# A new order for the opening's steps, a third pair run ahead, and the sums of the right factors on other ground

## The chip, the cores and the metric

One NeuronCore of a Trainium2 chip runs the whole program. The metric is the device time of one execution in microseconds (us); lower is better. The kernel before took 1624.2 us, the median of three runs from 1623.47 to 1624.24.

## The reference, cut to what matters

The program is one inference step of a one-layer streaming encoder on 1024 prompt rows and 8 x 16 sample rows, 1152 rows of 1024 channels in all. What the change touches is its first part, the norm and the input projection:

```python
def rmsnorm(x, g):
    xf = x.astype(jnp.float32)
    y = xf * lax.rsqrt(jnp.mean(xf * xf, axis=-1, keepdims=True) + EPS)
    return (y * g.astype(jnp.float32)).astype(x.dtype)

h = rmsnorm(x, g_pre_mix)
p = h @ w_in          # 1024 x 4352: queries, keys and values of two attentions, and two gates
```

Behind it come two attentions with position biases (two small tables are spread out in memory for them at the start), their projections, the gates, and a gated MLP. Those parts are the same in both kernels.

## The kernel before, in words

**Numbers in two parts.** Each fp32 operand of a matrix product is split into a high and a low part of a reduced format, so a product is three: high x high, high x low, low x high. ACT makes the high part (a copy), DVE the low part (a subtraction).

**The input projection** works on pairs of output tiles (`pairs`, twelve of them) with a scheme of Strassen's kind: seven products of half size stand in for eight, on sums of the halves of the weights (left factors, `left_factors`, L127 to L133) and of the input (right factors, `right_factors`, L429 on). The normed input, transposed, has channels on partitions; its halves by channels and by rows are b11, b12, b21 and b22, and t1, t2, t3 and t4 are the sums. A half has 576 rows, worked on as two chunks of 256 and 320 columns. One product of one left factor with one right factor and one chunk is twelve matmuls (`chunk_product`, L143).

**The opening** (L262 to L404). SP loads the nine blocks of 128 input rows (L279), with the left halves of the weights of the first two tiles among them (L285, behind blocks 1 and 3); seven buffers hold the nine blocks, so blocks 7 and 8 wait for the norms of blocks 0 and 1. For each block: `square` (ACT squares and sums, L296; DVE and GpSimd make the factor, L96 and L97), `norm` (DVE, L303 or L306), `transposed` (eight transposes on PE, L314, into two PSUM banks), `high` (ACT, L330) and, for rows of the first half, `low` (DVE, L335). Blocks 0 and 1 fill the first chunk of b11 and b21, blocks 2, 3 and half of 4 the second; the rest goes to b12 and b22 as plain fp32. The gains are spread over the partitions by PE, and `gp` is their copy by ACT (L350).

**The far products.** For the first tile of each of the first seven pairs, the two products with b11 and b21 are done ahead by the class `Away`: it splits the two left factors (L176, L177), `run(i, c)` is one product (i = 0 with b11, then i = 1 added onto it, chunk c), `copy(i, c)` copies the sum so far to `ia0h` or `ia1h` (L251), which are stored (L255, L195). `run(1, c)` waits for `copy(0, c)`. Tiles 0 and 1 are done within the opening, tile 2 (`Away(2)`) right behind it, tiles 3 to 6 after the pools of the opening are closed.

**What sets the order.** Within the opening the order on ACT, DVE and PE is written out by hand (`manual_schedule`). SP and GpSimd, and everything else in the program, are put in order by the framework's planner, which goes by dependencies and by its own estimates of times; each engine's and each queue's order is then fixed. Memory is a stack of pools: what is allocated after a pool is closed lies on the same addresses, and each tile waits for the last use of what lay beneath it (`reuse_waits="tile"`).

**The right factors.** After the opening, with its pools closed (input rows `xt` lowest, then `xn`, then small tables: `gp`, `eb`, `oh`, and `ea` last), the pools t3, t2, t1 and t4 are laid down in this order (L427). `sums` (plain fp32 for t3, t2 and t1) has the place that t4 takes later. `right_factors` is a generator of six steps: the sum for t3 with its parts; the sums for t1 and t2 (L438) with t2's parts (L211, L212); t1's parts; b22's parts; t4's sums (L438, L461) and parts; b12's parts. The first step is issued ahead of tiles 3 to 6, the others one by one in the first `tail`.

**The tail of a pair** (`tail`, L486): the product z with t3, x with t2, x with t1, x with b22, z with t4, each with the next left factor, which DVE sums in place in the raw weights `iw` (L127 to L133; loaded at L217) and ACT and DVE split (L176, L177, written `s_i`, `a_i`); in between DVE adds and copies out (`iu`, `iv`, `iw`, L191).

**After it** comes attention. Its first allocations on the same side are two buffers of raw rows (`karaw`, `q0raw`, ... loaded at L583), then four of bias tables, then the split rows of q and k. PE has dense gate tiles (`d`, L117 to L119) to fill in between the scores (`s`, L697).

Of the kernel before, what the change touches and what calls it, by code (L numbers as in the profile page):

```python
# [11 lines left out]
F32 = mybir.dt.float32  # L12
F32R = mybir.dt.float32r
# [5 lines left out]
P = 128  # L19
# [33 lines left out]
def encoder_step(ctx, tc, x, w_in, w_o, w_out, w_upg, w_down, kc, vc, state_conv, conv_w, conv_b,  # L53
# [104 lines left out]
    def chunk(c):  # L158
        return slice(c * widths[0], widths[0] + c * widths[1])
# [3 lines left out]
    with ExitStack() as ph:  # L163
# [7 lines left out]

        b12, b22 = [rq.tile([P, 4, 2 * CW], F32, name=n) for n in ("b12", "b22")]

        def split_left(src, name):
            sp = wop.tile([P, 2, 4, P], F32R, name=name, tag="wop")
            nc.scalar.activation(sp[:, 0], src, AF.Copy)  # L176
            nc.vector.tensor_tensor(sp[:, 1], src, fr(sp[:, 0]), op=ALU.subtract)  # L177
            return sp

        def two_chunks(name):  # L180
            return pa.tile([P, 2 * CW], F32, name=name, tag="a")

        def copy_out(ps, t):
            for c in range(2):
# [49 lines left out]
        class Away:  # L234


            def __init__(self, f, pool, early=False):
                self.f, self.pool, self.early = f, pool, early
                raw = away_weights(f)
                self.left = [split_left(raw[:, 4 * i:4 * i + 4], f"ih1{i}_{f}") for i in range(2)]  # L240
                self.out = [two_chunks(f"ia{i}h{f}") for i in range(2)]
                self.ps = [None, None]

            def run(self, i, c):
# [19 lines left out]
        with ExitStack() as pre:  # L264
# [73 lines left out]
            b = []  # L338

            def enter():  # L340
                b.append(Block(len(b)))
                b[-1].square()

            with tc.manual_schedule(engines={mybir.EngineType.Activation, mybir.EngineType.DVE, mybir.EngineType.PE}):
                enter()
                b[0].norm()
                enter()
                b[0].transposed()
                for i in range(2):
                    nc.scalar.activation(gp[:, i * 512:(i + 1) * 512], gps[i][:], AF.Copy)  # L350
                b[1].norm()
                b[0].high()
                b[0].low()
                w0 = Away(0, psx, True)
                b[1].transposed()
                b[1].high()
                b[1].low()
                enter()
                w0.run(0, 0)
                b[2].norm()  # L360
                w0.copy(0, 0)
                w1 = Away(1, psx, True)
                enter()
                b[2].transposed()
                b[2].high()
                w0.run(1, 0)
                b[2].low()
                b[3].norm()
                w0.copy(1, 0)
                enter()  # L370
                w1.run(0, 0)
                b[3].transposed()
                b[3].high()
                b[4].norm()
                w1.copy(0, 0)
                b[3].low()
                w1.run(1, 0)
                b[4].transposed()
                b[4].high()
                b[4].low()  # L380
                w1.copy(1, 0)
                enter()
                b[5].norm()
                w0.run(0, 1)
                w0.copy(0, 1)
                enter()
                w1.run(0, 1)
                b[5].transposed()
                b[5].high()
                w1.copy(0, 1)  # L390
                b[6].norm()
                w0.run(1, 1)
                enter()
                w0.copy(1, 1)
                b[6].transposed()
                b[6].high()
                b[7].norm()
                w1.run(1, 1)
                enter()
                w1.copy(1, 1)  # L400
                b[7].transposed()
                b[7].high()
                b[8].norm()
                b[8].transposed()  # L404
                b[8].high()

            Away(2, psx).all()


            rr = xs.tile([8, 2 * CLIP + 1], F32, name="rr")  # L410
# [13 lines left out]
            nc.scalar.activation(ea[:], pe[0:8, 0:EXT_A], AF.Copy, scale=-1.0)  # L424
            replicate(tab_a, ext_a, ea, EXT_A)

        tpool = [ph.enter_context(tc.tile_pool(name=f"t{i}", bufs=1, reuse_waits="tile")) for i in (3, 2, 1, 4)]  # L427

        def right_factors():  # L429

            for n, pool in zip(("t3", "t2", "t1"), tpool):
                rf[n] = pool.tile([P, 2, 4, 2 * CW], F32R, name=n)
            sums = tpool[3].tile([P, 2, 4, 2 * CW], F32, name="sums", tag="t")
            t3 = t2 = sums[:, 0]
            t1 = sums[:, 1]

            def sub(c, out, a, b):
                nc.vector.tensor_tensor(*[t[:, :, chunk(c)] for t in (out, a, b)], op=ALU.subtract)  # L438
# [23 lines left out]
            rf["t4"] = tpool[3].tile([P, 2, 4, 2 * CW], F32R, name="t4", tag="t")  # L462
# [1234 lines left out]
```

## Time and profile before

| | us |
|---|---|
| median of 3 runs | 1624.2 |
| the profiled execution | 1624.3 |
| its span | 1622.5 |
| PE busy | 1586.7 |
| DVE busy | 1104.8 |
| ACT busy | 726.9 |
| GpSimd busy | 213.5 |

The page's other lines on the whole run:

```profile
PE 84%; DVE 6%; ACT 4%; DMA 3%; issue 2%; SPq 0%; POOL 0%; DVEq 0%; POOLq 0%; ACTq 0%
DMA packets 93045, 205.94 MB, mean 127 GB/s; under 512 B 19321, under 2 KB 42793, under 8 KB 92914
```

The first is the chain of work that ended last, by engine: followed back from the last instruction, 84% of the span is work of PE. PE is TensorE's matmuls, PEld its weight loads, DVE VectorE, ACT ScalarE, POOL GpSimd, SP the engine that issues most DMAs. A row of the view in order of time has the start in us, the length, engine, line of the kernel, operation, output<-inputs, shapes, how many in a row, and in brackets the idle time of the engine before it with what ended it. In the view by stage a row has from:to, the length, busy us of each engine with the number of its instructions, TensorE's mean granted clock, the busy share of the DMA engines and GB/s.

### The profile page before, as it was taken

Reading aid. Unit: us, or ns where it says so; the run is one execution under the profiler, and the core shown is the slowest. Engines: PE = TensorE matmul, PEld = TensorE weight load, DVE = VectorE, ACT = ScalarE, POOL = GpSimd, SP = SyncE. Lnnn points to the kernel's source line nnn. Section 1 sums busy time; section 2 is a strip of 40 time slices with the busy share of each in tenths; the row PEclk is TensorE's granted clock in tenths of the full one; section 3 lists DMA queues with packets and bytes.
Section 4 is the critical chain, followed back from the end, with each engine's and each line's share of the span. In section 5 each row is a group of like instructions: output and inputs, shape, how many; then the busy total and the mean of one; then the engine's idle time right before and its main releaser. Section 6 shows DMA issues by size and latency. Waiting matters only on the chain.

```text
span 1622.5 us, 27938 instructions
## 1 busy us (share of the span) xinstructions
PE 1586.7 (98%) x10891; PEld 1465.6 (90%) x10891; DVE 1104.8 (68%) x2055; ACT 726.9 (45%) x1428; POOL 213.5 (13%) x287
## 2 busy tenths in 40 slices
PE   8999999999999999999999999999999999999998
PEld 6999999878788789988798999999999998888886
DVE  6976544677677755453499866676666767955987
ACT  7521233666555554332463344444444445434353
POOL 1000000211110003410002211221111211000002
PEclk9999999999999999999999999999999999999999
DMA  8654321754443265352155322122221218053023
GB/s 277 212 184 151 111 102 63 232 174 153 152 155 120 63 198 174 117 204 91 65 179 147 105 69 82 56 82 79 71 82 61 77 63 357 1 217 114 1 83 151
DMA packets 93045, 205.94 MB, mean 127 GB/s; under 512 B 19321, under 2 KB 42793, under 8 KB 92914
## 3 DMA queue, kind: packets, MB, share of 16 engines
q1 hardware_dynamic: 92640, 203.35, 36.6%
q8 instruction: 85, 1.39, 0.4%
q0 software_dynamic: 272, 0.81, 0.1%
q14 instruction: 46, 0.38, 0.1%
q10 hardware_dynamic: 2, 0.00, 0.0%
HBM read 147.61 MB, written 61.24 MB: 129 GB/s over the span
## 4 chain that ended last, share of the span: by engine, by line
PE 84%; DVE 6%; ACT 4%; DMA 3%; issue 2%; SPq 0%; POOL 0%; DVEq 0%; POOLq 0%; ACTq 0%
PE x L143 17%; PE z L143 8%; PE x L1479 8%; PE ix L143 7%; PE p L1479 6%; PE iz L143 4%; PE y L143 4%; PE o L754 2%; PE r L1127 2%; PE r L1129 2%; PE r L1128 2%; PE mp L965 2%; PE mp L967 2%; PE mp L966 2%; PE d L117 2%; PE d L119 2%
## 5 line engine op out<-in xcount | busy, mean ns | idle before, releaser
L143 PE MATMUL x<-xot,s 128*128 128x288 f32 x1152 | 158.2, 295 | 2.8 <-DVE s L1084 1.6
L143 PEld LDWEIGHTS x<-xot,s 128*128 128x128 f32 x1152 | 155.0, 188 | 3.4 <-DVE s L1084 1.9
L1479 PE MATMUL x<-wbp,zap 128*128 128x512 f32 x576 | 135.3, 389 | 0.0
L1479 PEld LDWEIGHTS x<-wbp,zap 128*128 128x128 f32 x576 | 108.1, 188 | 22.4
L1083 ACT ACTIVATE s<-uw 128x512 fp32r<-128x512 f32 x96 | 60.2, 627 | 102.7 <-issue 41.7
L705 ACT ACTIVATE p<-p,m 128x256 f32<-128x256 f32 (+4 forms) x128 | 74.8, 586 | 59.5 <-DVE m L700 59.5
L1479 PE MATMUL p<-wbp,zap 128*128 128x512 f32 x432 | 100.6, 389 | 0.0
L1479 PEld LDWEIGHTS p<-wbp,zap 128*128 128x128 f32 x432 | 81.0, 188 | 17.1 <-ACT yacc L1489 0.3
L1284 DVE SCALAR_TENSOR_TENSOR wk<-w,cw,wk 128x448 f32<-128x448 f32 (+1 forms) x144 | 86.2, 635 | 2.1 <-ACT wk L1282 1.2
L1084 DVE TENSOR_TENSOR s<-uw,s 128x512 fp32r<-128x512 f32 x96 | 66.8, 697 | 28.4 <-ACT s L1083 28.1
L1084 DVE TENSOR_TENSOR a<-uw,a 128x512 fp32r<-128x512 f32 x62 | 42.9, 692 | 62.7 <-ACT a L1083 61.5
L143 PE MATMUL z<-xot,a 128*128 128x288 f32 x576 | 80.9, 295 | 0.6 <-DVE a L1084 0.6
L143 PE MATMUL x<-xob,s 128*128 128x288 f32 x576 | 81.0, 295 | 0.3 <-DVE wk L1243 0.3
L143 PE MATMUL z<-xot,s 128*128 128x288 f32 x576 | 80.7, 295 | 0.0
L143 PEld LDWEIGHTS z<-xot,a 128*128 128x128 f32 x576 | 78.1, 188 | 0.9 <-DVE a L1084 0.9
L143 PEld LDWEIGHTS x<-xob,s 128*128 128x128 f32 x576 | 78.1, 188 | 0.7 <-DVE wk L1243 0.6
L143 PE MATMUL ix<-t,s_i 128*128 128x256 f32 (+1 forms) x576 | 78.1, 294 | 0.0
L143 PEld LDWEIGHTS z<-xot,s 128*128 128x128 f32 x576 | 78.1, 188 | 0.0
L143 PEld LDWEIGHTS ix<-t,s_i 128*128 128x128 f32 x576 | 76.7, 187 | 0.0
L176 ACT ACTIVATE s_i<-iw 128x512 fp32r<-128x512 f32 x48 | 30.0, 630 | 84.2 <-PE ix L143 40.7
L739 PE MATMUL pt<-ident,p 128*128 128x128 f32 x360 | 56.9, 282 | 8.4 <-ACT pk L743 5.5
L143 PE MATMUL x<-xob,a 128*128 128x288 f32 x456 | 63.9, 295 | 0.0
(638 smaller groups left out, 3838.5 us busy)
## 6 DMA issues: line engine op xcount, KB each, us to landing
uw<-in_w_upg SPq DMA_DIRECT2D x53, 512.0 KB, 3.7
iw<-in_w_in SPq DMA_DIRECT2D x24, 512.0 KB, 3.8
gg<-in_dr SPq DMA_DIRECT2D x16, 576.0 KB, 3.7
z_dr<-wk SPq DMA_DIRECT2D x23, 256.0 KB, 2.1
in_dr<-gt SPq DMA_DIRECT2D x30, 192.0 KB, 1.9
z_dr<-wk SPq DMA_DIRECT2D x23, 224.0 KB, 1.9
xt<-in_x SPq DMA_DIRECT2D x9, 512.0 KB, 7.8
oT<-o_dr SPq DMA_DIRECT2D x8, 576.0 KB, 5.1
```

The costliest lines, as they stand in the source:

```text
L117: nc.tensor.matmul(ps, w[:, 0, a], xg[0][:, b], start=start and k == 0, stop=False)
L119: nc.tensor.matmul(ps, w[:, 1, a], xg[0][:, b], start=False, stop=stop and k == nk - 1)
L143: nc.tensor.matmul(ps, w[:, i, k], right(j, c, k), start=first and n == 0, stop=last and n == len(todo) - 1, skip_group_check=True)
L705: nc.scalar.activation(p[h][:, 0:n], p[h][:, 0:n], AF.Exp, bias=least[h], scale=-1.0, accum_out=st.d[:, h, i:i + 1])
L739: nc.tensor.transpose(pt[:, h * nb + b], st.p[i][h][:, c:c + P], ident[:])
L754: nc.tensor.matmul(ps[r, c], k.vs[:, kb, r], p[h], start=n == 0, stop=n == len(st.pv) - 1)
L965: nc.tensor.matmul(ps[:], self.sp[:, 0, k], oT[k][:, 0, c], start=k % 4 == 0, stop=False)
L966: nc.tensor.matmul(ps[:], self.sp[:, 0, k], oT[k][:, 1, c], start=False, stop=False)
L1083: split["left"] = nc.scalar.activation(sp[:, 0], src, AF.Copy)
L1084: split["low"] = nc.vector.tensor_tensor(sp[:, 1], src, fr(sp[:, 0]), op=ALU.subtract)
L1284: nc.vector.scalar_tensor_tensor(out, src(t), cw[:, f, t:t + 1], out, op0=ALU.mult, op1=ALU.add)
L1479: nc.tensor.matmul(ps, z[:, i, k, c], w[:, j, k], start=first and n == 0, stop=last and n == 2, skip_group_check=True)
```

## The change

The opening's steps are written as one list, in a new order, and worked off by name. Tile 2 is run ahead in it like tiles 0 and 1, with two more small pools (`wop3`, `pa3`) for its split factors and its output, laid on top of the opening's; `Away(2).all()` behind the opening goes. Blocks 8 and 7 are taken ahead of 5 and 6. The pools of the right factors are laid down as t4, t3, t2, t1, so that `sums`, which has t4's place, lies lowest. In the first tail the second step of `right_factors` comes ahead of the product with t3, and the left factor of that product is queued on DVE behind the last of its subtractions (`issue_after`: an order on one engine); with that, each later step of `right_factors` stands one product earlier.

```diff
-        def split_left(src, name):
-            sp = wop.tile([P, 2, 4, P], F32R, name=name, tag="wop")
+        def split_left(src, name, pool=wop):
+            sp = pool.tile([P, 2, 4, P], F32R, name=name, tag="wop")
...
-            def __init__(self, f, pool, early=False):
+            def __init__(self, f, pool, early=False, wop=wop, pa=pa):
...
-            Away(2, psx).all()
+            wop3, pa3 = [pre.enter_context(tc.tile_pool(name=n, bufs=2)) for n in ("wop3", "pa3")]
...
+            def weights_of(f):
+                w[f] = Away(f, psx, True, wop if f < 2 else wop3, pa if f < 2 else pa3)
...
+                written = """
+                    enter.0 norm.0 enter.1 w.0 transposed.0 gp norm.1 high.0 transposed.1 low.0 enter.2 high.1 low.1
+                    run.0.0.0 norm.2 enter.3 w.1 norm.3 run.1.0.0 cp.0.0.0 enter.4 transposed.2 w.2 high.2 low.2
+                    transposed.3 run.2.0.0 norm.4 enter.8 run.0.1.0 high.3 cp.1.0.0 transposed.4 low.3 norm.8
+                    enter.7 high.4 low.4 cp.0.1.0 norm.7 run.1.1.0 transposed.8 enter.5 enter.6 norm.5 norm.6 high.8
+                    cp.1.1.0 run.0.0.1 transposed.7 cp.2.0.0 run.2.0.1 transposed.5 high.7 transposed.6 high.5
+                    run.1.0.1 high.6 run.2.1.0 cp.0.0.1 cp.1.0.1 run.0.1.1 run.1.1.1 cp.2.0.1 cp.1.1.1 run.2.1.1
+                    cp.2.1.0 cp.0.1.1 cp.2.1.1
+                """
...
-        tpool = [ph.enter_context(tc.tile_pool(name=f"t{i}", bufs=1, reuse_waits="tile")) for i in (3, 2, 1, 4)]
+        tpool = {i: ph.enter_context(tc.tile_pool(name=f"t{i}", bufs=1, reuse_waits="tile")) for i in (4, 3, 2, 1)}
...
-                nc.vector.tensor_tensor(*[t[:, :, chunk(c)] for t in (out, a, b)], op=ALU.subtract)
+                rf["sub"] = nc.vector.tensor_tensor(*[t[:, :, chunk(c)] for t in (out, a, b)], op=ALU.subtract)
...
-            product(zb, next(ops), of(rf["t3"]), True, False)
-            next(forms, None)
+            if f:
+                first = next(ops)
+            else:
+                next(forms)
+                with tc.issue_after(rf["sub"].ins):
+                    first = next(ops)
+            product(zb, first, of(rf["t3"]), True, False)
             product(xb, next(ops), of(rf["t2"]), a is not None, False)
             next(forms, None)
```

In the list, `run.f.i.c` and `cp.f.i.c` are product and copy of tile f, factor i, chunk c; `enter` is the square; `w.f` splits tile f's two left factors. Before, the order was, in the same words: enter.0 norm.0 enter.1 transposed.0 gp norm.1 high.0 low.0 w.0 transposed.1 high.1 low.1 enter.2 run.0.0.0 norm.2 cp.0.0.0 w.1 enter.3 transposed.2 high.2 run.0.1.0 low.2 norm.3 cp.0.1.0 enter.4 run.1.0.0 and so on, block by block up to block 8.

More of the change, by code (lines that the diff above doesn't have):

```diff
@@ L178, in split_left, with two_chunks @@
             return sp
-        def two_chunks(name):
-            return pa.tile([P, 2 * CW], F32, name=name, tag="a")
+        def two_chunks(name, pool=pa):
+            return pool.tile([P, 2 * CW], F32, name=name, tag="a")
         def copy_out(ps, t):
@@ L234, in encoder_step @@
         class Away:
-            def __init__(self, f, pool, early=False):
+            def __init__(self, f, pool, early=False, wop=wop, pa=pa):
                 self.f, self.pool, self.early = f, pool, early
                 raw = away_weights(f)
-                self.left = [split_left(raw[:, 4 * i:4 * i + 4], f"ih1{i}_{f}") for i in range(2)]
-                self.out = [two_chunks(f"ia{i}h{f}") for i in range(2)]
+                self.left = [split_left(raw[:, 4 * i:4 * i + 4], f"ih1{i}_{f}", wop) for i in range(2)]
+                self.out = [two_chunks(f"ia{i}h{f}", pa) for i in range(2)]
                 self.ps = [None, None]
@@ L336, in low @@
                                                     op=ALU.subtract)
[L338 to L348, printed above, removed]
+            wop3, pa3 = [pre.enter_context(tc.tile_pool(name=n, bufs=2)) for n in ("wop3", "pa3")]
@@ L349, in encoder_step, with enter, spread_weights @@
+            b, w = {}, {}
+            def enter(tb):
+                b[tb] = Block(tb)
+                b[tb].square()
+            def weights_of(f):
+                w[f] = Away(f, psx, True, wop if f < 2 else wop3, pa if f < 2 else pa3)
+            def spread_weights():
                 for i in range(2):
                     nc.scalar.activation(gp[:, i * 512:(i + 1) * 512], gps[i][:], AF.Copy)
[L351 to L405, printed above, removed]
@@ L407, in encoder_step @@
-            Away(2, psx).all()
+            steps = dict(enter=enter, gp=spread_weights, w=weights_of,
+                         run=lambda f, i, c: w[f].run(i, c), cp=lambda f, i, c: w[f].copy(i, c))
+            for name in ("norm", "transposed", "high", "low"):
+                steps[name] = lambda tb, name=name: getattr(b[tb], name)()
+            with tc.manual_schedule(engines={mybir.EngineType.Activation, mybir.EngineType.DVE, mybir.EngineType.PE}):
+                written = """
[7 more added lines that the diff above has]
+                """
+                for step in written.split():
+                    name, *args = step.split(".")
+                    steps[name](*map(int, args))
@@ L425, in encoder_step @@
             replicate(tab_a, ext_a, ea, EXT_A)
-        tpool = [ph.enter_context(tc.tile_pool(name=f"t{i}", bufs=1, reuse_waits="tile")) for i in (3, 2, 1, 4)]
+        tpool = {i: ph.enter_context(tc.tile_pool(name=f"t{i}", bufs=1, reuse_waits="tile")) for i in (4, 3, 2, 1)}
         def right_factors():
-            for n, pool in zip(("t3", "t2", "t1"), tpool):
-                rf[n] = pool.tile([P, 2, 4, 2 * CW], F32R, name=n)
-            sums = tpool[3].tile([P, 2, 4, 2 * CW], F32, name="sums", tag="t")
+            sums = tpool[4].tile([P, 2, 4, 2 * CW], F32, name="sums", tag="t")
+            for i in (3, 2, 1):
+                rf[f"t{i}"] = tpool[i].tile([P, 2, 4, 2 * CW], F32R, name=f"t{i}")
             t3 = t2 = sums[:, 0]
@@ L461, in right_factors @@
                 nc.vector.tensor_tensor(*[t[:, :, chunk(c)] for t in (b22, b22, part("b21", 1))], op=ALU.add)
-            rf["t4"] = tpool[3].tile([P, 2, 4, 2 * CW], F32R, name="t4", tag="t")
+            rf["t4"] = tpool[4].tile([P, 2, 4, 2 * CW], F32R, name="t4", tag="t")
             for c in range(2):
```

## The prediction

> **What bounds the kernel now.** I read the page first, then a table of stages, then each engine in order of time over the first 90 us. The page's first lines and the table by stage (us from:to, length, then busy us of PE, PEld, DVE, ACT, POOL):
>
> ```profile
> span 1622.5 us, 27938 instructions
> PE 1586.7 (98%) x10891; PEld 1465.6 (90%) x10891; DVE 1104.8 (68%) x2055; ACT 726.9 (45%) x1428; POOL 213.5 (13%) x287
> 0.00:38.00 38.00, 30.08 (x180) 25.18 (x181) 24.60 (x43) 27.85 (x56) 5.64 (x15) 1.00 0.80 280
> 38.00:68.20 30.20, 28.84 (x213) 27.75 (x211) 25.29 (x25) 21.64 (x38) 0.00 (x0) 1.00 0.82 276
> 68.20:86.00 17.80, 16.90 (x125) 16.62 (x126) 17.80 (x25) 5.84 (x9) 0.00 (x0) 1.00 0.28 86
> 86.00:295.00 209.00, 209.00 (x1581) 209.00 (x1582) 114.07 (x207) 59.09 (x111) 7.83 (x16) 1.00 0.37 131
> 295.00:600.00 305.00, 294.29 (x2537) 245.69 (x2537) 214.77 (x756) 171.92 (x481) 33.81 (x51) 0.99 0.46 146
> ```
>
> TensorE is the bound, and the change leaves its work alone, so it can only win idle time. Of the 35.8 us of idle PE (1622.5 - 1586.7), 7.9 lie in the opening, 1.4 in the far tiles after it, 0.9 in the first tail, none from 86 to 295, and 10.7 in attention. The first three sums, 10.2 us, are all that the change aims at. PE, in order of time (start, length, what, and in brackets the idle time before it and who ended it):
>
> ```profile
> 15.84 1.07 PE L314 MATMUL tp<-ident,xn 128*128 128x128 f32 x8 [1.47 <-DVE xn L306]
> 16.66 3.07 PE L143 MATMUL ixh<-xk,ih 128*128 128x256 f32 x24
> 37.71 5.88 PE L143 MATMUL ixh<-xk,ih 128*128 128x256 f32 x42
> 43.53 0.81 PE L422 MATMUL pe<-oh,tt 32*8 32x384 f32 x2
> 44.26 22.48 PE L143 MATMUL ixh<-xk,ih 128*128 128x256 f32 x168
> 68.10 3.44 PE L143 MATMUL ixh<-xk,ih 128*128 128x256 f32 x24 [1.36 <-ACT ia0h L251]
> 71.38 3.33 PE L143 MATMUL iz<-t,s_i 128*128 128x256 f32 x24
> 85.82 2.91 PE L143 MATMUL iz<-t,a_i 128*128 128x256 f32 x20 [0.90 <-DVE a_i L177]
> 88.56 3.33 PE L143 MATMUL iz<-t,s_i 128*128 128x256 f32 x24
> 104.43 3.33 PE L143 MATMUL iz<-t,s_i 128*128 128x256 f32 x24
> ```
>
> From 88.56 to 104.43 lies one undisturbed tail: ten chunk products in 15.87 us, 1.59 each; by their 256 and 320 columns that is 1.41 and 1.76. A block's eight transposes take 0.82 up to the next start (15.84 to 16.66); with the slower first matmul behind them I count 0.9.
>
> **Part 1, the new opening (gain 1.6).** The list lets tile 2's left half be split on ACT behind `transposed.2` and ahead of `high.2`. That adds a wait: the split needs tile 2's weights from memory. Queued behind it on ACT are `high.2`, the square of block 8, `high.3` and a copy, and PE waits for it in `run.2.0.0`. When do the weights land? SP issues them behind all nine input tiles:
>
> ```profile
> 10.49 0.90 SPq L225 DMA_DIRECT2D iwh<-in_w_in  x2
> 0.00:18.30 18.30, 12.90 (x54) 9.31 (x55) 10.95 (x22) 12.49 (x22) 2.90 (x10) 1.00 0.91 344
> DMA to landing us min/median/max: 3.8/5.7/9.9
> 14.68 1.14 ACT L176 ACTIVATE ih<-iwh 128x512 fp32r<-128x512 f32 x2
> 15.60 1.29 DVE L177 TENSOR_TENSOR ih<-iwh,ih 128x512 fp32r<-128x512 f32 x2
> ```
>
> By 18.3 us 344 GB/s have moved 6.30 MB, twelve transfers of 512 KB, and tile 2's is the twelfth (nine of x, two weights before). The slowest weight transfer took 9.9 us, so with the second issue at about 11.0 that one landed by 20.9; one transfer less, 1.3 us at 0.52 MB and about 410 GB/s, gives 19.4 for tile 2's (estimate). The new norm of block 1 stands behind tile 0's splits and so is about 0.8 us later, and with it block 8's load, but the DMA engines are full then (share 0.91 in the row above), so I cost that at nothing; without that cover it costs its 0.8.
>
> Up to there PE has finished the transposes of blocks 0 to 3 and two products, and it waits. From 19.4: high part 0.62, low part 0.69, hand-overs 0.2, so the products of tile 2 run from 20.9. After that the list holds four products of 256 columns, six of 320 and the transposes of five blocks: 4 x 1.41 + 6 x 1.76 + 5 x 0.9 = 20.7, with 0.3 for small waits: done at 41.9. ACT keeps up: behind the split stand seven high parts of about 1.0, four squares of 1.0 and copies of 0.3, some 15 us, so that its last high part is out near 35, when PE has five products left. Before, the same work (two tiles, nine blocks, tile 2) ends at 43.53, where the small table's product starts. Gain 1.6. Each us by which the weights land earlier or later moves it by a us: 3.1 if they pass block 8's rows on SP, -0.5 if they land at 21.5.
>
> **Part 2, sums over the raw rows, and forms one step earlier (gain 1.7 + 1.3).** DVE and ACT, same columns:
>
> ```profile
> 39.62 1.23 DVE L212 TENSOR_TENSOR xk<-b,xk 128x1024 fp32r<-128x1024 f32 x1 [1.67 <-ACT xk L211]
> 48.23 2.63 DVE L438 TENSOR_TENSOR sums<-b,b 128x1024 f32<-128x1024 f32 x2 [1.85 <-DMA tab_a<-ea]
> 63.24 0.69 DVE L127 TENSOR_TENSOR iw<-iw 128x512 f32<-128x512 f32 x1 [1.23 <-DMA iw<-in_w_in]
> 66.50 1.27 ACT L211 ACTIVATE t<-sums 128x1280 fp32r<-128x1280 f32 x1 [1.53 <-DVE sums L438]
> 67.68 0.69 ACT L251 ACTIVATE ia0h<-ixh 128x256 f32<-128x256 f32 x2
> ```
>
> The first sum starts at 48.23, when the small table `ea` under it has been read out. DVE then works without a pause until it waits 1.23 us for pair 0's weights at L127, with the second sum queued behind; ACT's t2 part waits for that sum (1.53), the copy `ia0h` stands behind it on ACT, and PE waits 1.36 us for the copy at 68.10. Once more late, DVE gives the split of `a_i` 0.9 us late at 85.82.
>
> Now the sums lie over raw rows, free when the last norm is done (before 35); their inputs are complete at about 35 too. So DVE starts the sums some 13 us earlier and uses the time it had spent waiting. `issue_after` puts L127 behind all these sums: what it makes late is pair 0's own left splits, which PE wants only at about 68, and the weights were there at 63.2. From 43.53 to 71.38 PE needs 27.85 us; its work in that is 0.73 (the table) and sixteen products of 1.59, 26.1. The first tail takes 88.56 - 71.38 = 17.18 instead of 15.87. So 1.7 and 1.3 can go; what is late next is nothing that I can see, since DVE's work from 35 to that last split is twelve passes like the one at 48.23 (six sums, six low parts) of 2.6, seventeen pieces of left factors of 0.6 and some 3 us of adds, 44 us, ready at 79, and PE asks for it eight products after 68.0, at 80.7. Bounds: the shift of forms also lets t4's sums (1.2 to 1.5 us each) stand before a copy that PE waits for, so 0.3 to 1.7 and 0 to 1.3. I take the upper ends, since the row that causes them, 48.23, goes.
>
> **Part 3, what now lies lowest (cost 0.7).** The order of the pools changes from t3, t2, t1, t4 to t4, t3, t2, t1. The next stage lays its raw rows first, at the lowest place. SP's longest waits there, its issue, its landing, and PE:
>
> ```profile
> SPq L583 <- PE iz L143: 2.2, 1, 2.2
> 282.33 0.32 SPq L583 DMA_DIRECT2D karaw<-in_dr  x1
> DMA to landing us min/median/max: 3.6/3.6/3.7
> 278.96 3.33 PE L143 MATMUL iz<-t,s_i 128*128 128x256 f32 x24
> 291.66 3.33 PE L143 MATMUL iz<-t,a_i 128*128 128x256 f32 x24
> 294.83 0.34 PE L117 MATMUL d<-xk,w12s 128*128 128x384 f32 x1
> 295.35 0.34 PE L117 MATMUL d<-xk,w12s 128*128 128x384 f32 x1
> 295.62 0.33 PE L697 MATMUL s<-kah,q0h 64*128 64x128 f32 x2
> L591 ACT ACTIVATE kah<-karaw x2: 621/622/624, 289.0 to 289.5; 128x512 fp32r<-128x512 f32 x2
> ```
>
> `karaw` is loaded the moment the last product with t3 ends (282.3). With t4 there it waits for the last product of all, 295.0: 12.7 us later. On SP stand behind it `q0raw`, the bias tables and the out-copy of k. In time from that product's end: issue 0.1, landing 3.7, two splits of k 1.1 (289.0 to 289.5 and 0.6), q's first 0.5: the first scores at 5.4, where they now come at 0.6 (295.62), 4.8 later; those that need q's low part on DVE, another 0.7, are 5.5 later. I count 5.2. Dense tiles hide this: tile 12 is split and ready (294.83), and its 72 matmuls at 0.17 (three from 294.83 to 295.35) are 12 us of work that has no need of the rows. What is drawn forward is missing later, but scores then find less before them. Price 0 with the cover, 5.2 without; 0.7 taken, for a part of a hand-over missed.
>
> A stall there could cost more than itself:
>
> ```profile
> PE pt L739 <- DVE pk L741: 2.4, 1, 2.4
> 410.00:420.00 10.00, 7.02 (x44) 5.23 (x43) 7.44 (x21) 3.19 (x12) 2.68 (x1) 0.83 0.82 257
> ```
>
> In attention PE idled 2.4 us, and the mean granted clock of that window fell to 0.83, worth 10 x 0.17 = 1.7 us of clock. So a bare stall of 5.2 can take another 1.7: 6.9. The Trainium skill ("TensorE: Matmul & The Clock Gate", Part 1: The HAM clock gate) has half clock after an idle window of about 3.4 us in a free-running count; by that rule 2.4 us need not have done it, and the trace shows that it did. A part stall of 3.4 us would end at 1624.2 - 4.6 + 3.4 = 1623.0 by the rule, and at 1624.7 by the trace.
>
> **Sum.** 1.6 + 1.7 + 1.3 - 0.7 = 3.9. The profiled execution took 1624.3 (span 1622.5 and 1.8 around it), so 1620.4; it lies 0.1 above the median of the runs, 1624.2, hence 1620.3. From 0.2% of the time, 3.2 us, a measurement tells a difference.
>
> **Rivals.**
> *The raw rows' lateness decides (slower).* Part 3 without cover: parts 1 and 2 give 4.6, the bare stall with its clock takes 6.9: 1626.5. For it: SP's wait above is exact, and PE keeps its order, so scores placed too early in it stop all dense work. Against: dense work is there, and four of its matmuls already stand before the first scores. It ends slower than before once the stall passes 4.6, and beyond 0.2% only if the opening also falls short. Chance 0.15.
> *Only the opening wins.* Another wait stands in for the 1.36 and the 0.90, for example ACT's parts of 1.27 in front of copies, or the shifted forms: 1.6 + 0.6 - 0.7 = 1.5, so 1622.7. Against it is DVE's earlier start. Chance 0.15.
> *Weights late.* Tile 2's weights land 2 us later, behind small tables: 3.9 - 2.1 = 1.8, so 1622.4. Against: they are issued ahead of these now. Chance 0.1.
> *It does not do what it says:* sums still wait for a table, and parts 2's gain is gone, 1.6 - 0.7: 1623.3. Chance 0.05.
> *Weights early,* landing at 17.9: 1618.8, chance 0.1.
> The forecast proper keeps 0.45.
>
> **Numbers.** The order of everything outside the list is planned anew, so a stall like the 2.4 with its 1.7 can go or come; that and the early weights set the low end, 1617.3. The high end, 1625.3, takes in the bare stall without the clock (1624.2 - 4.6 + 5.2 = 1624.8) with 0.5 for a smaller gain. Faster by over 0.2%: most of the forecast and the early weights, 0.51; slower: some of the first rival and ill luck, 0.11; within: 0.38.
>
> **What would show it.** In the changed profile: ACT idle about 3 us before tile 2's split near 19.4; the last product of tile 2 ending near 42; the first sum starting near 35 and not at 48; no idle before 68, z of pair 0 near 68.0 and of pair 1 near 83.9; `karaw` issued just after the last `iz<-t,a_i`, with dense matmuls between that and the first scores. I am wrong if z of pair 0 comes after 70, or if PE's idle time in attention grows by over 2 us.

## The result, and the profile after

The change made the kernel slower, by half a per cent.

| | before | after |
|---|---|---|
| median of 6 runs each (us) | 1624.2 | 1633.1 (1630.3 to 1637.6) |
| ratio to before | | 1.0052, interval 1.0033 to 1.0070 |
| profiled execution | 1624.3 | 1630.8 |
| its span | 1622.5 | 1629.0 |
| PE busy | 1586.7 | 1593.0 |

The profile after, by stage, in the columns of the table in the prediction:

```profile
span 1629.0 us, 27929 instructions
0.00:38.00 38.00, 32.74 (x201) 28.43 (x202) 28.20 (x47) 30.94 (x61) 6.46 (x15) 1.00 0.66 242
38.00:68.20 30.20, 25.78 (x179) 24.68 (x179) 27.15 (x26) 18.92 (x32) 0.00 (x0) 0.92 0.87 290
68.20:86.00 17.80, 17.80 (x129) 17.80 (x129) 14.50 (x23) 5.74 (x11) 0.00 (x0) 0.94 0.69 242
```

The first stage is better by 2.7 us of PE work, and the second one worse: 25.8 busy instead of 28.8, and at a clock of 0.92. PE in order of time says where:

```profile
41.00 0.81 PE L385 MATMUL pe<-oh,tt 32*8 32x384 f32 x2
41.74 19.31 PE L143 MATMUL ixh<-xk,ih 128*128 128x256 f32 x144
65.47 8.83 PE L143 MATMUL ixh<-xk,ih 128*128 128x256 f32 x48 [4.42 <-ACT ih L176]
74.13 3.33 PE L143 MATMUL iz<-t,s_i 128*128 128x256 f32 x24
90.00 2.16 PE L143 MATMUL iz<-t,s_i 128*128 128x256 f32 x16
```

The table's product, which ends the opening, starts at 41.00 instead of 43.53, and tiles 3, 4 and 5 run 2.5 us ahead of before. Then PE stands still for 4.42 us, and the four products that follow need 8.66 (65.47 to 74.13) where 2 x 1.41 + 2 x 1.76 = 6.3 would do at full clock. z of pair 0 starts 2.75 later than before, not 3.4 earlier. The first tail then takes 15.87 (90.00 - 74.13), which is an undisturbed one: the 0.90 at 85.82 is gone. From pair 1 to the end of the projection the kernel is 1.44 behind, without change.

PE waits for tile 6's split on ACT, and that for the weights. The chain of waits says it in its own words:

```profile
57.91 0.43 ACT ia0h L251
58.43 6.33 DMA iwh<-in_w_in
64.79 0.64 ACT ih L176
65.47 8.83 PE ixh L143 x48
```

The transfer is not slow (6.33 us; before, a weight transfer took 3.8 to 9.9), it is issued late. SP's queue before, and after:

```profile
41.80 0.38 SPq L225 DMA_DIRECT2D iwh<-in_w_in  x1
45.01 0.29 SPq L89 DMA_DIRECT2D tab_a<-ea  x1
48.12 4.96 SPq L92 DMA_DIRECT2D ext_a<-tab_a  x8
54.96 1.76 SPq L217 DMA_DIRECT2D iw<-in_w_in  x2
```

```profile
45.52 0.99 SPq L89 DMA_DIRECT2D tab_a<-ea  x1
52.27 4.96 SPq L92 DMA_DIRECT2D ext_a<-tab_a  x8
58.43 1.01 SPq L225 DMA_DIRECT2D iwh<-in_w_in  x1
60.50 1.34 SPq L217 DMA_DIRECT2D iw<-in_w_in  x2
```

Before, tile 6's weights (`iwh`, L225) are issued at 41.80, ahead of the small table `tab_a`. After, they stand behind the table, behind its eight spreads to `ext_a`, which wait until the table has landed (52.27), and behind two stores of results. Where the spread does not stand in front of it (six of the runs below) this load is issued at 49.5 to 50.2, so 8 to 9 of the 16.6 us by which it is late are the spread's; the rest was not followed further. Pair 0's weights (`iw`, L217) go 5.5 us later too. Nobody moved a line for that: SP's order is the planner's, and it is planned anew.

The second loss is at the start of attention. SP and PE there, after:

```profile
296.46 0.32 SPq L552 DMA_DIRECT2D karaw<-in_dr  x1
297.36 0.42 SPq L552 DMA_DIRECT2D q0raw<-in_dr  x1
```

```profile
296.27 0.34 PE L117 MATMUL d<-xk,w12s 128*128 128x384 f32 x1
304.48 0.49 PE L666 MATMUL s<-kah,q0h 64*128 64x128 f32 x4 [1.12 <-ACT q0h L560]
```

The raw rows are loaded when the last product ends, as forecast. The first scores come 8.2 us after the first dense matmul, where it was 0.8, and dense work covers that up to 1.12 us of idle time. Yet the stretch becomes longer by more than that. Three dense tiles mark the way through it, and the third (`w8s`) begins, before and after:

```profile
352.66 0.42 PE L117 MATMUL d<-xk,w8s 128*128 128x384 f32 x1
```

```profile
358.73 0.42 PE L117 MATMUL d<-xk,w8s 128*128 128x384 f32 x1
```

From the first matmul of the first (`w12s`) to the first of the third it is 57.83 us before (from 294.83) and 62.46 after (from 296.27). Only 0.88 of these 4.63 us is more idle time on PE (1.63 before, 2.51 after); the other 3.75 stand in the profile as busy time, for as many matmuls (514 and 513) at full clock. The ends of matmuls are modelled there, so short waits between them can count as busy; that these are the scores, which now find too few dense matmuls between them, is my reading and not shown. By there the kernel is 6.1 behind (1.4 + 4.6). A stall of 2.3 us before 589 is missing in the new plan, so it is 4.8 at the first product of the next stage (599.41 and 604.17) and 6.5 at the end, 1.3 of which are lost between 819 and 856 and 0.4 up to 1501, in parts that are the same in both kernels.

### The profile page after: what moved, and what is told of

Its sections match the earlier page's. It is cut to its first block, busy times and chain, and to the rows that moved or that the text cites. A ratio compares the mean times of both kernels' runs of the same rounds, so it can differ in the third digit from the quotient of the medians.

```text
span 1629.0 us, 27929 instructions
## 1 busy us (share of the span) xinstructions
PE 1593.0 (98%) x10891; PEld 1469.3 (90%) x10891; DVE 1102.5 (68%) x2055; ACT 725.5 (45%) x1428; POOL 215.8 (13%) x287
## 4 chain that ended last, share of the span: by engine, by line
PE 88%; DVE 4%; DMA 3%; ACT 3%; issue 1%; POOL 0%; SPq 0%; DVEq 0%; POOLq 0%; ACTq 0%
PE x L143 17%; PE z L143 8%; PE ix L143 8%; PE x L1448 8%; PE p L1448 6%; PE iz L143 5%; PE y L143 4%; PE ixh L143 2%; PE o L723 2%; PE r L1096 2%; PE r L1098 2%; PE r L1097 2%; PE pt L708 2%; PE d L117 2%; PE s L666 2%; PE mp L935 2%
## 5 line engine op out<-in xcount | busy, mean ns | idle before, releaser
L1053 DVE TENSOR_TENSOR s<-uw,s 128x512 fp32r<-128x512 f32 x96 | 66.8, 697 | 28.4 <-ACT s L1052 28.1
```

The source lines that it names most:

```text
L1053: split["low"] = nc.vector.tensor_tensor(sp[:, 1], src, fr(sp[:, 0]), op=ALU.subtract)
```

## Theories, and a table of all runs

**Theory.** Two costs outweigh a gain that is real: (1) tile 6's weights are issued late on SP, and the idle time that this makes also halves PE's clock for a while; (2) the raw rows of attention lie over t4 and come late. **Rivals.** (a) The sums and forms that now stand early on DVE and ACT make the tiles late, so that earlier weights would not help; (b) the new list itself is bad for what follows; (c) it is mostly the clock, and idle time on PE by itself.

The kernels e0 to e15 were timed in five rounds (e5 in three), six to twelve executions each, beside the kernel before on the same chip: e1, e2, e3 and e5 on one chip, e6 to e9 on a second, e0 and e13 to e15 on a third. The first two rows are those of the result above. The ratio is to the kernel before in the same rounds, so ratios of different chips are to be compared with care. The times of PE are those of the profiled execution: the table's product, z of pair 0, z of pair 1, and the way from `w12s` to `w8s`.

| kernel | pe | z 0 | z 1 | w12s to w8s | ratio to before (interval) |
|---|---|---|---|---|---|
| before | 43.53 | 71.38 | 88.56 | 57.8 | 1 |
| after | 41.00 | 74.13 | 90.00 | 62.5 | 1.0052 (1.0033 to 1.0070) |
| e1_pools_3421 | 41.41 | 74.29 | 90.16 | 59.8 | 1.0023 (1.0013 to 1.0033) |
| e2_load_first | 41.19 | 71.04 | 89.66 | 62.2 | 1.0033 (1.0019 to 1.0047) |
| e3_load_first_3421 | 41.41 | 70.38 | 89.00 | 59.7 | 1.0018 (1.0008 to 1.0027) |
| e5_keep_busy | 41.14 | 73.30 | 89.17 | 62.1 | 1.0024 (1.0014 to 1.0034) |
| e6_pools_forms_alone | 44.75 | 75.52 | 91.39 | 62.5 | 1.0037 (1.0022 to 1.0052) |
| e7_opening_alone | 42.35 | 73.85 | 95.07 | 58.5 | 1.0039 (1.0026 to 1.0052) |
| e8_ext_a_pool | 41.23 | 69.39 | 85.37 | 62.1 | 1.0041 (1.0026 to 1.0055) |
| e9_ext_a_pool_3421 | 41.91 | 73.21 | 89.08 | 59.9 | 1.0005 (0.9995 to 1.0015) |
| e0_after_again | 41.70 | 73.51 | 89.38 | 62.2 | 1.0044 (1.0029 to 1.0060) |
| e13_spread_last | 41.77 | 68.57 | 84.57 | 62.2 | 1.0017 (1.0002 to 1.0031) |
| e14_spread_last_3421 | 41.02 | 68.18 | 84.14 | 59.5 | 0.9979 (0.9967 to 0.9991) |
| e15_before_spread_last | 44.35 | 70.58 | 86.44 | 58.5 | 0.9989 (0.9977 to 1.0002) |

## The raw rows: another order of the pools

```diff
-tpool = {i: ... for i in (4, 3, 2, 1)}
+tpool = {i: ... for i in (3, 4, 2, 1)}
```

> One edit to the changed kernel: the pools of the right factors lie as t3, t4, t2, t1, so t3 is lowest again and the sums lie over raw rows and norms above it. Theory (two prices, tile 6's weights late on SP, and attention's raw rows late because they lie over t4): the far tiles stay as in the changed kernel (PE idle 4.4 us before tile 6, z of pair 0 near 74.1), but the load of karaw no longer waits for the last product, the first scores come within 2 us of that product's end instead of 8, and the time falls by about 4.6 us. Rival (the loss in attention comes from the new plan of its order, not from where its rows lie): first scores still 6 to 8 us behind, time within 1 us of the changed kernel.

Measured: 1.0023, where the changed kernel had 1.0052 beside other runs. The start of the kernel is as in the changed one (z of pair 1 at 90.16); the first scores come 2.0 us after the first dense matmul, and the way to `w8s` falls from 62.5 to 59.8. The profiled execution does not keep that: it has lost it again by the next stage (604.77, against 604.17 after), some 1.7 us to the clock at the stall of 2.40 told of at the end and more to a wait of 2.15 before 594, and its span, 1628.9, is that of the changed kernel. The medians of runs on one chip do show the edit: it is worth 2.9, 4.5 and 4.9 us in the three pairs below (e2 and e3, e8 and e9, e13 and e14). The rows are loaded in time again, but what is split out of them is not:

```profile
283.92 0.32 SPq L552 DMA_DIRECT2D karaw<-in_dr  x1
```

```profile
296.62 1.16 ACT L560 ACTIVATE kah<-karaw 128x512 fp32r<-128x512 f32 x2 [2.73 <-PE iz L143]
```

The raw rows lie over t3 now, the split rows over t4, and the split waits 2.73 us for the last product with t4. Some 1 to 2 of the 4.6 stay; by my reading that is for this wait. All seven profiles with t4 lowest have 62.1 to 62.5 on this way, the four with t3 lowest 59.5 to 59.9, and the three with the old pools 57.8 to 58.5: no kernel leaves its group, whatever its opening does. So with t4 lowest the way costs 4 us more than with the old pools, and moving t4 alone takes 2.5 of them away: that much of cost 2 is shown to be t4 lying under the raw rows. The last 1.5 go with the new pools and the early forms together, since no run has the old pools with the early forms.

## Tile 6's weights: first in SP's queue, then off it

**The load ahead of the spread.** The small table `ea` gets a pool of its own, and its spread is queued on SP behind tile 6's load; the second kernel has t3 lowest as well.

```diff
+late = right_pool("late")
-ea = xs.tile([8, EXT_A], F32, name="ea")
+ea = late.tile([8, EXT_A], F32, name="ea")
-replicate(tab_a, ext_a, ea, EXT_A)
...
+with tc.issue_after(rf["load"].ins):      # behind tile 6's load
+    replicate(tab_a, ext_a, ea, EXT_A)
```

> The changed kernel with the spreading of the second small table queued on SP behind the load of tile 6's weights; the table's row ea gets a place of its own so that it can wait. Theory: the weights land before 58, PE does not idle before tile 6, the granted clock stays at 1.0 there, z of pair 0 starts near 67.2 instead of 74.1, and the profile's time falls by 6.9 us to about 1623.9. Rival (DVE and ACT are held up by the earlier sums and forms, and the load is only the last of several waits): another wait of 2 us or more takes its place before 74, and the time falls by less than 4.

> Both edits together. Theory: 6.9 and 4.6 add up, about 1619.3, 5 us below the kernel before, with z of pair 0 near 67.2 and the first scores within 2 us of the last projection product. Rival (the two share a cause, or the early gain is given back later): above 1622.

Measured: 1.0033 and 1.0018, much less than the theory gave, and as its rival had it: z of pair 0 comes at 71.04 and 70.38 and not at 67.2. Tile 6 runs without a wait, but PE stops one tile later. SP's queue of the first kernel, and PE:

```profile
49.49 0.43 SPq L226 DMA_DIRECT2D iwh<-in_w_in  x1
52.64 0.38 SPq L218 DMA_DIRECT2D iw<-in_w_in  x1
60.44 1.81 SPq L92 DMA_DIRECT2D ext_a<-tab_a  x3
62.54 0.34 SPq L218 DMA_DIRECT2D iw<-in_w_in  x1
```

```profile
71.04 0.50 PE L143 MATMUL iz<-t,s_i 128*128 128x256 f32 x2 [3.42 <-ACT s_i L177]
72.38 4.74 PE L143 MATMUL iz<-t,s_i 128*128 128x256 f32 x22 [0.84 <-DVE s_i L178]
```

The spread now stands between the two halves of pair 0's weights, and the second half goes at 62.54. The wait has changed its place and not its kind. The theory of cost 1 was too narrow: it is not tile 6's load but whatever weights come behind the eight spreads.

**The spread from GpSimd's queue.** So the spread went to another queue:

```diff
-nc.sync.dma_start(ext[h], ...)
+(nc.gpsimd if n == EXT_A else nc.sync).dma_start(ext[h], ...)
```

> The changed kernel, with the eight spreads of the small table a (tab_a to ext_a) issued from GpSimd's queue and not SP's. Theory (SP's order is the whole cause of the stall at 61 and of the one that took its place at pair 0): tile 6's weights are issued near 49, pair 0's near 53, both land before they are wanted; no idle over 0.5 between 41 and 72, no half clock there; z of pair 0 at 67.2 to 68, z of pair 1 at 83.2 to 84 (-4.6 to -5.3); the raw rows cost 4.6 and end is -0.5 to +0.5, 1624. Rival (with the weights there, the splits and copies on ACT and DVE are the next limit): z of pair 0 not before 70, z of pair 1 -2 or later, end +2 to +3, 1627.

> Both cures: ext_a's spread from GpSimd's queue and t3 as the lowest of the four pools, so that the raw rows do not wait for t4. Theory: projection as in the run with the queue alone (-4.6 to -5.3 at z of pair 1), raw rows +1.2, so end -3 to -4, 1620 to 1621.5; what the attention stage's stalls do may move it by 2 either way. Rival (ACT and DVE are the next limit): z of pair 1 -2, end near -1 to 0, 1623 to 1624.

Measured: 1.0041 and 1.0005, where the time of before and a gain of 3 to 4 us were expected. In the first kernel z of pair 1 comes at 85.37 (-3.2), short of the expected -4.6; in the second, with the same queues, at 89.08 (+0.5). The second one's PE, DVE and ACT:

```profile
68.62 4.75 PE L143 MATMUL ixh<-xk,ih 128*128 128x256 f32 x24 [3.29 <-ACT ia0h L251]
```

```profile
63.94 0.69 DVE L127 TENSOR_TENSOR iw<-iw 128x512 f32<-128x512 f32 x1 [4.02 <-DMA iw<-in_w_in]
```

```profile
64.72 0.63 ACT L176 ACTIVATE s_i<-iw 128x512 fp32r<-128x512 f32 x1 [5.46 <-DVE iw L127]
65.25 0.69 ACT L251 ACTIVATE ia1h<-ixh 128x256 f32<-128x256 f32 x2
68.20 0.36 ACT L251 ACTIVATE ia0h<-ixh 128x256 f32<-128x256 f32 x1
```

Read from below: PE waits for ACT's copies of tiles 5 and 6; these stand on ACT behind the split of pair 0's first left factor; that waits for the sum on DVE (L127); and that, at the head of DVE's queue, for pair 0's weights. They were issued at 53.35 and 53.79 and landed at 62.0 and 63.8, 8.7 and 10.0 us later, with the spread under way beside them; in the first kernel they were issued some 0.7 us earlier, with the same spread beside them, took 5.1 and 7.7 and had landed at 60.8. Why they took longer in one than in the other is open. With sums done early, DVE reaches L127 at 60, before the weights are there, and in-order queues carry that over to PE. Rival (a) is right in part: the early forms do not make tiles late by their work, but they bring the wait for the weights in front of the copies. The first kernel lost another 2.4 us in parts behind attention, 1.5 of it in the clock event told of at the end; and its profiled execution, 1627.9, is the fastest of its eight, whose median is 1631.3, so that most of what the others lost stands in no trace.

**The spread out of the way altogether**, behind the weights of pair 2, in fact some 30 us later and not the 50 of the expectation (it begins at 82.80, after it was 52.27 in the changed kernel). It is wanted at 286 (bias tables) and not before.

```diff
 late = right_pool("late"), ea = late.tile(...)          # as above
+for f in range(len(pairs)):
+    start = head_back(f) if f < NA else head(f)
+    if f == 2:
+        with tc.issue_after(rf["load"].ins):            # pair 2's weights
+            replicate(tab_a, ext_a, ea, EXT_A)
+    tail(f, *start, forms)
```

> The changed kernel, with the spread of the small table a (tab_a, then eight ext_a) put on SP behind the weights of pair 2, some 50 later; ea has a place of its own for that. Nothing of it stands ahead of the weights of tile 6, pair 0 or pair 1, and nothing of it is in memory's way while they are loaded. Theory (what is left of the stall in the run with GpSimd's queue is pair 0's weights, which took 8 to 10 us to land beside the spread, DVE waiting at L127 with ACT's copies behind it): tile 6's weights issued near 49, pair 0's near 52, landed within 5; no idle over 0.5 between 41 and 72; z of pair 0 at 67.2 to 68.5 and z of pair 1 at 83 to 84.5 (-4.1 to -5.5 against before); raw rows +4.6; end 0 to -1, 1624. Rival (splits and copies of ACT and DVE limit even then): PE waits 1 to 3 before pair 0, z of pair 1 at -2 to -3, end +2.

> The same, and t3 as the lowest of the four pools. Theory: z of pair 1 at -4.1 to -5.5, raw rows +1.2 to +1.7 and no more, so end -2.5 to -4, 0.9975 to 0.9985 of before. Rival (ACT and DVE limit): end -0.5 to -1.5.

> The kernel before, untouched in its opening, pools and forms, with the same move of the spread alone. It takes away the lock that the first sum had on the small table (48.23) as well. If the late weights and the late sum were all that before lost after its opening: no 1.36 at 68.1, first tail 16 to 16.5, z of pair 1 at -1.5 to -2.7, no lateness of the raw rows, end -1.5 to -2.7. If it brings nothing, the gain of the two runs above belongs to the change itself and not to the moved spread.

> The changed kernel as it is, on the chip of the other three runs, to set them beside it: 4 to 7 us above before here too, idle of 3.5 to 4.5 before tile 6, z of pair 0 at 73.5 to 74.5.

Measured, medians on one chip: before 1625.9, the changed kernel 1631.6, with the spread last 1627.4, with t3 lowest too 1622.5, and the kernel before with the spread last 1624.0. PE of the kernel with both cures, and what SP issues ahead of it:

```profile
41.02 0.81 PE L386 MATMUL pe<-oh,tt 32*8 32x384 f32 x2
41.75 24.29 PE L143 MATMUL ixh<-xk,ih 128*128 128x256 f32 x180
66.31 2.03 PE L143 MATMUL ixh<-xk,ih 128*128 128x320 f32 x12 [0.27 <-ACT ia0h L252]
68.18 3.33 PE L143 MATMUL iz<-t,s_i 128*128 128x256 f32 x24
84.14 3.33 PE L143 MATMUL iz<-t,s_i 128*128 128x256 f32 x24
```

```profile
50.11 0.38 SPq L226 DMA_DIRECT2D iwh<-in_w_in  x1
50.96 0.33 SPq L218 DMA_DIRECT2D iw<-in_w_in  x1
52.42 0.42 SPq L218 DMA_DIRECT2D iw<-in_w_in  x1
```

Pair 0's weights land 5.9 and 6.3 us after their issue (near 56.9 and 58.7), and DVE takes them up at 59.73 without a wait. From the table's product to z of pair 0 there are 27.16 us, of which 0.27 are idle time, and z of pair 1 is 4.42 ahead of before. So the 5.7 us between before and after come apart into 4.2 for the weights behind the spread (1631.6 to 1627.4), 4.9 for the pools (1627.4 to 1622.5), and a gain of 3.4 that was hidden under both (1625.9 to 1622.5); by the intervals in the table each of these is good to some 2 us. The kernel before gains from the moved spread as well: its wait of 1.36 is gone, z of pair 1 comes 2.1 earlier, as its theory had it, and it wins 1.9, though its interval just reaches 1. So the 4.2 holds some of what the kernel before loses too. The changed kernel with both cures lies 1.5 below that one, but their intervals overlap, and these runs do not separate them.

## Which part of the change makes the load late

Two kernels with half of the change each: the old opening list with the new pools and early forms, and the new list with the old pools and forms.

```diff
 e6: the opening list, Away(2).all(): as before;   tpool, right_factors, tail: as after
 e7: the opening list, tile 2 in it: as after;     tpool, right_factors, tail: as before
```

> The kernel before with the new pools, the raw-row sums and the early forms, but with the old opening list. Theory (the new list is what moves the weights of tile 6 behind the table spread on SP): here that load keeps its old early place, so no idle before tile 6 and no half clock near 63; z of pair 0 at 70.0 (71.38 less the 1.36), first tail 15.9, so z of pair 1 at 85.9 (-2.7 against before); the raw rows that now lie over t4 then cost 4.6, end +1.9, 1626 to 1627. Rival (the sums that now stand early on DVE, and not the list, make tile 6 or pair 0 late): an idle of 3 to 4 us before tile 6 or pair 0 here too, z of pair 1 at +1 to +2, end +6, about 1630.

> The new opening list alone, with the old order of pools and the old place of the forms. Theory: PE ends the opening at 41.0 as in the changed kernel, then idles about 4.4 before tile 6 (weights issued near 58, behind ext_a) with 3.4 lost to half clock; z of pair 0 near 74, and the first tail 17.2 as before or less, z of pair 1 at +1.5 to +2.7; no lateness of the raw rows, end +1.5 to +2.7, 1626 to 1627. Rival (list is good, all the loss comes from the pools and forms): no idle before tile 6, z of pair 0 at -2.5, end 1621 to 1622.

Measured: 1.0037 and 1.0039. Each half alone is slower than before. With the new list alone tile 6's load stands behind the spread again (58.62) and PE idles 3.27 before tile 6; so the list does that, as the theory said, and rival (b) is right so far. But the first tail takes 21.2 instead of 17.2, which neither theory had: DVE, with the sums of t4 and their parts still before it, gives the last part of t4 0.86 and the split of `a_i` 0.92 late, one shortly after the other, and 3.4 us at half clock follow (88 to 96: 0.79 on the mean). With the pools and forms alone the load is early (42.81), no wait is before tile 6, and yet z of pair 0 is 4.1 late, 1.2 of it from the opening, 1.4 from more idle time and 1.5 from half clock behind it:

```profile
70.72 4.96 PE L143 MATMUL ixh<-xk,ih 128*128 128x256 f32 x24 [2.75 <-ACT ia0h L251]
```

This is the chain of L127 once more: here the weights of pair 0 were issued behind the spread (56.41) as before (54.96) and were there at 65.7 instead of 63.2, and DVE, with its sums done early, waits 3.64 at L127 where it waited 1.23. The old place of the sums had hidden part of that wait.

Which entry of the list moves the load is open.

## How much of it is the clock

To hold the clock, 36 useless matmuls were put in front of tile 6's first product.

```diff
+if self.f == 6 and i == 0 and c == 0:
+    for n in range(36):
+        nc.tensor.matmul(self.ps[c], <b11>, <b11>, start=True, stop=True)
```

> The changed kernel with 36 matmuls of no use (0.118 us each, 4.2 us) ahead of tile 6's first product, into the bank that this product then overwrites; they need nothing that is late. Theory: the wait for the weights stays, but PE is not idle in it, so the granted clock does not fall: z of pair 0 near 70.7, the profile's time about 3.4 us lower, and the runs lie closer together. Rival (the clock falls for another reason, or the useless matmuls only add themselves): z of pair 0 at 74 or later.

Measured: 1.0024. PE, in order of time:

```profile
61.02 4.47 PE L251 MATMUL ixh<-xk 128*128 128x256 f32 x36
65.69 0.50 PE L143 MATMUL ixh<-xk,ih 128*128 128x256 f32 x2 [0.20 <-ACT ih L176]
70.02 3.44 PE L143 MATMUL ixh<-xk,ih 128*128 128x256 f32 x24 [0.40 <-ACT ia0h L256]
73.30 3.33 PE L143 MATMUL iz<-t,s_i 128*128 128x256 f32 x24
```

The mean granted clock from 60 to 76 is 1.00 here, and from 63 to 71 it is 0.57 in the changed kernel: 3.4 us of clock lost, of which the part beside idle time costs nothing; the expectation counted all of it, while the products had lost 2.3. But z of pair 0 comes only 0.8 earlier, at 73.30 and not at 70.7: at full clock the products of tile 6 wait for splits and copies instead (0.20, 0.23 and 0.40). In this place the clock's loss lay over other waits; so rival (c) falls for this place. The profiled execution is 3.7 us shorter than that of the changed kernel, about as expected, but 2.0 of that arise between 845 and 863, where the changed kernel waits for DVE (0.99 and 0.34) and this one does not, and it is the fastest of its ten; their median is 1630.6. The ratio, 1.0024, comes from other rounds than that of the changed kernel, and I read no more from it.

## Why the prediction was wrong

**The opening (part 1): right, and better than forecast.** The table's product comes at 41.00 against 41.9 forecast. In the eleven profiles with the new list it comes at 41.0 to 42.4, in the three with the old one at 43.5 to 44.8, so the gain is 2.4 to 3.5 between runs on one chip, 2.5 here, and not 1.6. Tile 2's weights were the mis-sized term: the split starts at 18.47 instead of 19.4, ACT having waited 2.46 for them, and the end of the opening comes 0.9 earlier with it.

**The sums (part 2): right in the tail, half right ahead of it, wrong in what comes next.** The first sum starts at 32.96, and the tail is an undisturbed one (1.3). With the weights in time z of pair 0 is at 68.18 and z of pair 1 at 84.14, near the 68.0 and 83.9 of the forecast, but in part by luck: from the table's product to z of pair 0 it takes 27.16 and not the 26.1 of the sum, so 0.7 of the 1.7 is gained there, and the opening, 0.9 early, makes up for it. The step that failed is "what is late next is nothing that I can see". It looked at DVE's work alone. It took "the weights were there at 63.2" from a queue that the change was going to have planned anew, and asked neither when the new plan issues tile 6's and pair 0's weights (64.8 and 66.8 is when they landed) nor what waits on ACT behind L127. The row was there to warn: SP issued `iwh` at 41.80 just ahead of the table and its eight spreads, which hold the queue until 53.1. Behind them, tile 6's load came 16.6 us later.

**The raw rows (part 3): the mechanism right, the size wrong.** 0.7 was taken and 4 to 5 measured, near the bare 5.2 that the prediction had as its upper bound without cover. The first scores came 7.4 us later against the first dense matmul, where 4.8 to 5.5 was counted. The dense matmuls did cover the wait, all but 1.12 us, and still the stretch became 4.63 longer. "Price 0 with the cover" was the wrong bound: the prediction itself says that what is drawn forward is missing later, and put that at nothing because scores then find less before them. That this is where the time went fits the runs, but which waits it made is open. The second row also came later than the 0.5 that was counted for q: ACT starts its split at 303.80, 3.1 after that of k, having waited 1.58 for it.

**The rival that won** was none of those named: the one on the slower side, raw rows late, holds half of it. By its price, 6.9 against 4.6 of gain, it came to 1626.5. "Weights late" was there for tile 2 alone, where they came early; the same question was not put to tile 6 and pair 0. (A slip that changes nothing: the low end, 1618.8 less the 1.7 of a stall, is 1617.1 and not 1617.3.)

**The clock.** The Trainium skill ("TensorE: Matmul & The Clock Gate", Part 1: The HAM clock gate) has half clock after an idle window of about 3.4 us; the prediction set the trace's 2.4 against it. The runs side with the trace: after 2.75 and 3.29 us of idle time (e6 and e9), and after 2.58 with 0.84 close behind (e3), 3.4 us at half clock followed.

## What to carry to other kernels

When the order of one engine is changed by hand and the rest is planned, look at the in-order queues that nobody touched: for each load whose consumer is near the critical path, ask when it is issued and what could slip in front of it; a burst of transfers that is wanted much later (here 286 against 48) belongs behind them by an explicit order. A stall that is taken away on one engine brings the next wait of that engine forward, and everything queued behind that wait. And the order in which pools are laid down decides when the next stage can start: what is used last should not lie under what is loaded first.

## What the runs showed of the clock

Idle time on PE can be followed by half clock in pieces of 3.4 us, and one and the same idle time brings none, one or two of them. In steps of 2 us the clock of the changed kernel reads 0.50 from 64 to 70; over a longer window the length follows from the mean, so 0.57 over 8 us is 3.4 us lost, or 6.9 at half clock. In attention every profiled execution has a stall of 2.40 to 2.42 us. Half clock follows for 3.4 us in five of fourteen, for 6.8 in eight, and not at all in one, e15_before_spread_last. That stage in before, in e0_after_again and in e15_before_spread_last (us from:to, and the granted clock third from the end):

```profile
415.00:423.00 8.00, 7.41 (x47) 5.94 (x47) 4.51 (x17) 4.60 (x15) 0.00 (x0) 0.79 0.62 228
```

```profile
420.00:428.00 8.00, 7.38 (x38) 5.67 (x39) 4.39 (x15) 3.86 (x13) 0.00 (x0) 0.57 0.63 228
814.00:826.00 12.00, 10.10 (x65) 9.87 (x64) 8.48 (x11) 6.93 (x14) 1.48 (x2) 0.86 0.33 99
```

```profile
415.00:423.00 8.00, 7.10 (x53) 5.88 (x55) 5.17 (x19) 5.29 (x16) 0.00 (x0) 1.00 0.67 232
```

A later wait of 1.90, near 810, which all have, costs clock in two of fourteen: in e0_after_again (0.86 over the twelve us above) and in e8_ext_a_pool. The 2.31 of before at 587 cost none, nor did those of 1.99 to 2.15 at the same place in e1, e2 and e7, nor single waits of 1.17 to 1.65 us from 66 to 874 in any profile, but the 0.86 and 0.92 close together in e7_opening_alone did. So 1.7 to 3.4 us of a profile's time can hang on whether such a stall costs clock, for which these traces show no rule: with the same stall of 2.40, e15_before_spread_last has a profile of 1621.5 and a median of 1624.0.
